# The layer norm of a segment ranked 800 operations later, and the first five weight blocks kept in DRAM like the others

## The chip, the cores and the metric

The kernel runs on one core of a Trainium2 chip. The metric is the device time of one execution in microseconds; several runs are taken and their median is quoted. One more execution was recorded by the hardware profiler, and every row below comes from that one.

## The reference

One layer of a decoder with two token mixers on the same input, for a prompt of 2048 tokens and for 8 short sequences of 4 tokens ("decode"). Cut to what matters here:

```python
u = x * (1 + scale) + shift                 # scale, shift, gate from c @ w_ada
proj = u @ w_in                             # 1024 -> 9344 columns
y_a = rwkv7(proj...)                        # branch A: 16 heads of 64, a recurrent state
y_b = retention(proj...)                    # branch B: 4 heads, chunks of 128 tokens
merged = sigmoid(g_a) * o_a + sigmoid(g_b) * o_b
sub = merged @ w_out
y = norm(ALPHA * x + gate * sub) * ln_gain + ln_bias
```

All data are float32. The last line, with the multiplication of `sub` by `gate`, is the stage whose rank changes.

## The kernel before, in words

**Segments and heads.** The prompt is cut into 4 segments of 512 tokens. A segment begins with `uprep`, which loads x in 8 slices, forms u and splits it into a high part `uh` and a low part `ul` (the products are done in three passes: high by high, high by low, low by high). Segment 1 also carries the 32 decode tokens, so each of its slices is split in three pieces and its matmuls are twice 272 columns. Then come four rounds, one for each retention head. A round does two pairs of heads of branch A (`pair_inputs`, five blocks of projection each; then `half`, `solve`, `half`), one head of branch B (`ret_proj`, two `ret_gate`, `ret_math`), and the output projection of the round before (`outproj`), because the order of a round is `P0 J R G0 D P1 N O G1 S J M00 M01 M10`, with `O` the output projection. `D` is the decode computation, once, in the first round of segment 2.

**Output.** `outproj` adds its products into one buffer, `zt` (128 partitions by 4 by 1024). There is only one `zt`; the first round of the next segment overwrites it in its own output projection (`A.copy(out=z, in_=pz)`, one round after). After the fourth round `outproj` calls `final`: for each half of the columns and each of 4 token blocks GpSimd multiplies `zt` by the gate, VectorE adds the scaled x and takes the statistics; then VectorE normalises, GpSimd multiplies by the gain, VectorE adds the bias, and the rows are stored. That is 16 GpSimd and 32 large VectorE operations and 76 operations in all. Because of the order of a round, the `final` of segments 0, 1 and 2 runs in the first round of segments 1, 2 and 3. The last segment ends with another function, `outproj_last`, which the change does not touch.

**Weights.** A block of `w_in` is loaded as two float32 halves into `fx` buffers (there are 4). ScalarE casts a half to its high part, GpSimd subtracts to get the low part (`split`). The result, 1 MB for a block in a `ww` buffer (3 of them), is stored to DRAM by a transfer on the SP queue (`wpair`, the `cache`) and loaded again in later segments by one transfer that GpSimd issues. Five blocks, `FIRST = 24, 41, 57, 0, 8`, are loaded and split ahead, during the first `uprep` (`ahead`), into buffers of several kinds. These five are not stored in segment 0; segment 1 loads and splits them again and stores them then.

**The order.** All operations are first recorded with a rank, their number in program order plus an offset (`prio_off`; `uprep` of segments 1 to 3 has -700). A planner then lays them out on a model of the engines: whenever an engine is free in the model, it takes the available operation with the lowest rank. It prefers one kind of matmul to another within 500 ranks. The engines execute the resulting lists in order; so do SP's and GpSimd's queues of transfers. Since every instruction is issued from one place, all rows say L529 and must be told apart by tile names.

In program order, the `final` of segment 0 holds operations 9021 to 9096 of 31541; then come `ret_gate`, `ret_math` and the second `half, solve, half` of that round, up to 9750, and `pair_inputs` of the next round. The next overwrite of `zt` is in the `outproj` at 11187. For segment 1 the numbers are 18194 to 18269 and 19866, for segment 2 they are 25296 to 25371 and 26974.

Of the kernel before, what the change touches and what calls it, by code (L numbers as in the profile page):

```python
# [10 lines left out]
F32 = mybir.dt.float32  # L11
# [51 lines left out]
RUN = 2  # L63
UPO = 700
DOFF = 0
JBN = 3, 2, 2, 2, 2
JB=dict(zip(("AR", "W", "UV", "BT", "Z"), JBN))
NPP,NSM = 3,3
# [758 lines left out]
class Mixer:  # L827
# [277 lines left out]
    def proj(self, s, blk, dst, to=None):  # L1105
        dec = s == self.dseg
        n = 2 if dec else 1
        pts = [self.early.pop(blk, None) or self.pp.tile([128, 512], F32, tag="pp", name="pp") for _ in range(n)]
        if (blk, 0) in self.first:
            ws = [self.first.pop((blk, g)) for g in range(2)]  # L1110
        else:
            ws = self.wpair("wf", (blk,), [self.i["wf"][blk, g] for g in range(2)], s < self.ns - 1,
                            to if to is not None and to.t.tag.tag in EARLY else None)
        for g in range(2):
            hi, lo = ws[g]
            for k4 in range(4):
                k = g * 4 + k4
                ks = slice(k4 * 128, (k4 + 1) * 128)
                for q, (w, u) in enumerate(((hi, self.uh), (hi, self.ul), (lo, self.uh))):
                    for j in range(n):  # L1120
                        mv = u[k][:, j * 272:(j + 1) * 272] if dec else u[k][:, 0:512]
                        if to is not None and to.t.tag.tag in LATE and to.t.first is None and k == q == j == 0 and not (s == 0 and blk in FIRST):
                            self.pl.reserve = (to,)
                        self.pl.hold = self.begin if s == 0 and k == 0 and blk in FIRST else None
                        self.T.matmul(pts[j][:, 0:272] if dec else pts[j], lhsT=w[:, ks], rhs=mv,
                                      start=(k == 0 and q == 0), stop=(k == 7 and q == 2))
                        self.pl.hold = None
        if dec:
            t = self.tiny(ND)
            for j in range(2):  # L1130
                self.A.copy(out=t[:, j * 16:(j + 1) * 16], in_=pts[j][:, 256 - 256 * j:272 - 256 * j])
            self.nc.sync.dma_start(out=self.ddram[:, dst], in_=t)
            return [(pts[0][:, 0:256], 0, 256), (pts[1][:, 16:272], 256, 256)]
        return [(pts[0], 0, 512)]
# [673 lines left out]
    def outproj(self, s, h, dec):  # L1808
        T, V, A, G = self.T, self.V, self.A, self.G
        last = s == self.ns - 1  # L1810
        if last and h == NH_B - 1:
            return self.outproj_last(s)
        if h == 0:
            self.zt = self.j1.tile([128, 4, D], F32, tag="zt", name="zt")
        for q in range(4):
            qs = slice(q * 256, (q + 1) * 256)
            if last:
                if q % 2 == 0:
                    wg = self.ww.tile([128, 2, 2, 512], F32R, tag="ww", name="ww")
                hi, lo = self.split(self.i["wo"][h, q], wg[:, q % 2, 0], wg[:, q % 2, 1], gate=q)  # L1820
            else:
                if q % 2 == 0:
                    wp = self.wpair("wo", (h, q), [self.i["wo"][h, q + g] for g in range(2)], s < self.ns - 2)
                hi, lo = wp[q % 2]
            ws = [slice(k * 256, (k + 1) * 256) for k in range(2)]
            for i2 in range(2):
                pz = self.pp.tile([128, 2, 256], F32, tag="pp", name="pp")
                for j in range(2):
                    i = i2 * 2 + j
                    n = 0  # L1830
                    for k in (1, 0):
                        mh, ml = self.mg[k]
                        for w, m in ((hi, mh), (hi, ml), (lo, mh)):
                            T.matmul(pz[:, j], lhsT=m[:, i * 128:(i + 1) * 128], rhs=w[:, ws[k]], start=n == 0, stop=n == 5)
                            n += 1
                z = self.zt[:, 2 * i2:2 * i2 + 2, qs]
                if h == 0 and last:
                    x = self.fx((128, 2, 256))
                    r = s * SEG + i2 * 256
                    self.nc.sync.dma_start(out=x, in_=self.i["xp"][r:r + 256, qs].rearrange("(j p) c -> p j c", j=2))  # L1840
                    V.scalar_tensor_tensor(out=z, in0=x, scalar=ALPHA, in1=pz, op0=MUL, op1=ADD)
                elif h == 0:
                    A.copy(out=z, in_=pz)
                else:
                    V.tensor_tensor(out=z, in0=pz, in1=z, op=ADD)
            if dec:
                self.outproj_dec(h, [(q, (hi, lo))])
        self.mg = {}
        if h == NH_B - 1:
            rows = [slice(s * SEG + i * 128, s * SEG + (i + 1) * 128) for i in range(4)]  # L1850
            self.final([[self.zt[:, i, 0:512], self.zt[:, i, 512:1024]] for i in range(4)], 128,
                       [self.i["xp"][r] for r in rows], [self.o["yp"][r] for r in rows], False)

    def outproj_last(self, s):

# [108 lines left out]
    def run(self):  # L1964
# [3 lines left out]
        for s in range(self.ns):  # L1968
# [8 lines left out]
            for h in range(NH_B):  # L1977
                last = s == self.ns - 1 and h == NH_B - 1
                gate = {}
                for step in (LAST if last else ORDER if s + h else BEGIN).split():  # L1980
# [28 lines left out]
                    elif step[0] == "D" and s == self.dseg + 1 and h == 0:  # L2009
                        self.pl.prio_off = DOFF  # L2010
                        self.decode()
# [28 lines left out]
```

## Time and profile before

| | us |
|---|---|
| median of 3 runs | 3134.05 |
| lowest and highest | 3130.12, 3137.01 |
| the profiled execution | 3128.51 |
| its span, first to last instruction | 3126.7 |

The mean granted TensorE clock over the span is 0.969 of full speed. PE is TensorE's matmuls, DVE is VectorE, ACT ScalarE, POOL GpSimd, SP the queue of transfers. A wait is named by who waited and for what: "PE pp <- DVE t" is TensorE waiting to write an accumulator `pp` until VectorE has written `t`, that is, has read the accumulator out.

### The profile page before, as it was taken

The numbers are of one execution on the slowest core, as the hardware profiler recorded it, in microseconds if no ns is written. First come the engines' busy times: TensorE is split into PE (matmuls) and PEld (weight loads), VectorE is DVE, ScalarE is ACT, GpSimd is POOL, SyncE is SP. The second block draws the span as 40 slices with busy tenths as digits, with TensorE's granted clock in tenths as the row PEclk, the third lists the DMA queues.
The fourth block names the chain that finished last, engine by engine and source line by source line (L and its number), as shares of the span: only waits on it lengthen the run. The fifth ranks groups of instructions, "written<-read, shape, count | busy, mean of one in ns | idle before, by whom it ended". The sixth has DMA issues, their size and how long they took to land. (4 is left out here: it accounts for less than half of the span.)

```text
span 3126.7 us, 63842 instructions
## 1 busy us (share of the span) xinstructions
PE 2896.4 (93%) x24700; PEld 2332.8 (75%) x24700; DVE 1919.9 (61%) x4748; ACT 1566.2 (50%) x3859; POOL 1048.3 (34%) x1451
## 2 busy tenths in 40 slices
PE   8999999989989999989998788999999989998996
PEld 5777778768888989879774466777787766777675
DVE  3566676666576365565665575565676675566666
ACT  4466755656436455453541045554555346454652
POOL 4554456433252131222210242232232442334232
PEclk9999999999999999999998789999999999999997
DMA  8564556534362433425344432333343452533321
GB/s 303 199 229 161 175 191 222 191 127 160 117 226 99 130 108 112 137 94 178 136 128 150 158 110 97 135 124 122 131 152 124 156 176 79 172 119 122 108 83 38
DMA packets 132792, 451.86 MB, mean 145 GB/s; under 512 B 30500, under 2 KB 41636, under 8 KB 92680
## 3 DMA queue, kind: packets, MB, share of 16 engines
q0 software_dynamic: 33120, 241.19, 22.5%
q1 hardware_dynamic: 99368, 206.58, 19.6%
q8 instruction: 195, 3.19, 0.4%
q14 instruction: 109, 0.89, 0.1%
HBM read 345.83 MB, written 101.88 MB: 143 GB/s over the span
## 5 line engine op out<-in xcount | busy, mean ns | idle before, releaser
L529 PE MATMUL pp<-uh,ww 128*128 128x512 f32 (+1 forms) x5152 | 1476.8, 366 | 43.8 <-DMA ww<-wc_wf 15.6
L529 PEld LDWEIGHTS pp<-uh,ww 128*128 128x128 f32 x5152 | 880.5, 190 | 168.3 <-DVE t L529 22.7
L529 PE MATMUL pp<-ul,ww 128*128 128x512 f32 (+1 forms) x2576 | 883.7, 364 | 0.1
L529 PEld LDWEIGHTS pp<-ul,ww 128*128 128x128 f32 x2576 | 468.6, 190 | 54.5 <-issue 1.4
L529 POOL DMA_DIRECT2D ww<-wc_wf x190 | 109.0, 574 | 625.3 <-PE pp L529 514.5
L529 POOL TENSOR_TENSOR ww<-fx,ww 128x512 fp32r<-128x512 f32 x178 | 234.4, 1330 | 211.5 <-ACT ww L529 197.7
L529 ACT CAST ZX<-sm 128x512 f16<-128x512 f32 (+1 forms) x363 | 206.3, 572 | 91.0 <-PE sm L529 86.7
L529 ACT ACTIVATE tn<-UV,PL 64x64 f32<-64x64 f32 x512 | 177.0, 346 | 117.9 <-DVE UV L529 95.8
L529 POOL TENSOR_TENSOR t<-t,t 128x256 fp32r<-128x256 f32 (+2 forms) x160 | 150.6, 943 | 199.5 <-ACT t L529 189.1
L529 DVE TENSOR_TENSOR HH<-sm,lev 128x512 f16<-128x512 f32 (+1 forms) x165 | 111.3, 674 | 160.5 <-PE sm L529 159.7
L529 PE MATMUL pp<-ww,mh 128*128 128x256 f32 x960 | 190.4, 290 | 3.5 <-ACT zt L529 1.9
L529 DVE TENSOR_SCALAR UV<-ch 64x64 f32<-64x64 f32 x256 | 55.2, 227 | 207.3 <-ACT UV L529 184.4
L529 POOL TENSOR_TENSOR tn<-tn,mhalf 128x4 f32<-128x4 f32 (+2 forms) x108 | 100.9, 935 | 216.1 <-DVE tn L529 214.1
L529 PE MATMUL pp<-ww,uh 128*128 128x256 f32 x1024 | 171.6, 291 | 1.4 <-DVE t L529 0.8
L529 ACT CAST bdZ<-sm 64x512 f16<-64x512 f32 (+1 forms) x264 | 149.5, 566 | 24.9 <-PE sm L529 20.1
L529 PEld LDWEIGHTS pp<-ww,mh 128*128 128x128 f32 x960 | 154.9, 193 | 8.0 <-ACT zt L529 2.3
L529 PEld LDWEIGHTS pp<-ww,uh 128*128 128x128 f32 x1024 | 140.7, 190 | 5.3 <-ACT UV L529 0.7
L529 DVE SCALAR_TENSOR_TENSOR UV<-ch,PL,tn 64x64 f32<-64x64 f32 x384 | 108.7, 283 | 57.4 <-PE ch L529 47.5
L529 ACT ACTIVATE t<-pp 128x512 f32<-128x512 f32 (+1 forms) x160 | 80.6, 519 | 118.3 <-PE pp L529 100.7
L529 PE MATMUL pp<-ww,ml 128*128 128x256 f32 x480 | 138.4, 289 | 0.1
L529 ACT ACTIVATE UV<-ch 64x64 f32<-64x64 f32 x256 | 51.6, 215 | 171.3 <-PE yy L529 137.8
L529 DVE COPY bdH<-HH 64x512 f16<-64x512 f16 (+1 forms) x396 | 124.7, 315 | 8.5
(255 smaller groups left out, 5420.1 us busy)
## 6 DMA issues: line engine op xcount, KB each, us to landing
ww<-wc_wf POOLq DMA_DIRECT2D x190, 1024.0 KB, 5.1
wc_wf<-ww SPq DMA_DIRECT2D x65, 1024.0 KB, 5.4
fx<-in_wf SPq DMA_DIRECT2D x140, 256.0 KB, 3.4
ww<-wc_wv POOLq DMA_DIRECT2D x24, 1024.0 KB, 5.2
ww<-wc_wo POOLq DMA_DIRECT2D x16, 1024.0 KB, 5.1
wa<-in_wa SPq DMA_DIRECT2D x16, 512.0 KB, 5.2
wc_wv<-ww SPq DMA_DIRECT2D x8, 1024.0 KB, 5.5
fx<-in_wo SPq DMA_DIRECT2D x32, 256.0 KB, 2.8
```

Of the source, the lines that this page charges most:

```text
L529: op.fn = lambda: real(*[res(x) for x in a], **{k: res(x) for k, x in kw.items()})
```

## The change

The `final` that follows the last output projection of segments 0, 1 and 2 gets 800 added to the rank of each of its operations, its transfers on the SP queue included. And each of the five blocks loaded first is stored to DRAM in segment 0, as four transfers of 256 KB (its halves lie in different buffers), after its matmuls in program order; from segment 1 on it is loaded from there.

```diff
+FOFF = 800
...
-        if (blk, 0) in self.first:
+        early = (blk, 0) in self.first
+        if early:
             ws = [self.first.pop((blk, g)) for g in range(2)]
...
+        if early:
+            key = "wf", blk
+            self.cache[key] = self.drp.tile([128, 2, 2, 512], F32, name="wc_wf_%d" % blk)
+            for g in range(2):
+                for q in range(2):
+                    self.nc.sync.dma_start(out=self.cache[key][:, g, q], in_=ws[g][q].bitcast(F32))
...
         if h == NH_B - 1:
             rows = [slice(s * SEG + i * 128, s * SEG + (i + 1) * 128) for i in range(4)]
+            off, self.pl.prio_off = self.pl.prio_off, FOFF
             self.final([[self.zt[:, i, 0:512], self.zt[:, i, 512:1024]] for i in range(4)], 128,
                        [self.i["xp"][r] for r in rows], [self.o["yp"][r] for r in rows], False)
+            self.pl.prio_off = off
```

## Rows read from the trace of the kernel before

**Rows 1.** The page: busy us, share of the span and instructions of each engine.

```profile
PE 2896.4 (93%) x24700; PEld 2332.8 (75%) x24700; DVE 1919.9 (61%) x4748; ACT 1566.2 (50%) x3859; POOL 1048.3 (34%) x1451
```

**Rows 2.** Stretches: busy us of PE, PEld, DVE, ACT, POOL; PEclk; DMA share, GB/s.

```profile
685.00:715.00 30.00, 15.88 (x88) 13.12 (x87) 28.32 (x69) 15.66 (x32) 15.38 (x20) 0.72 0.50 146
885.00:925.00 40.00, 27.98 (x207) 27.36 (x207) 35.57 (x52) 9.01 (x28) 30.44 (x34) 0.87 0.69 234
1780.00:1840.00 60.00, 39.53 (x246) 31.68 (x245) 52.15 (x96) 21.34 (x42) 38.62 (x40) 0.77 0.47 154
2480.00:2540.00 60.00, 45.60 (x196) 35.84 (x194) 43.80 (x64) 14.14 (x27) 38.20 (x43) 0.89 0.69 228
1455.00:1480.00 25.00, 24.66 (x157) 21.19 (x157) 19.60 (x40) 14.24 (x34) 8.14 (x17) 1.00 0.56 183
```

**Rows 3.** Columns as in rows 2, the stretches whose clock fell furthest.

```profile
700.00:715.00 15.00, 11.84 (x69) 10.50 (x70) 13.79 (x28) 7.92 (x16) 8.19 (x9) 0.59 0.39 101
915.00:920.00 5.00, 2.96 (x13) 2.96 (x14) 4.99 (x10) 1.48 (x2) 3.31 (x3) 0.50 0.36 109
1790.00:1810.00 20.00, 11.80 (x47) 8.60 (x48) 16.09 (x31) 6.07 (x14) 16.66 (x20) 0.55 0.35 117
2520.00:2530.00 10.00, 3.07 (x7) 2.48 (x8) 8.52 (x15) 2.58 (x5) 4.80 (x5) 0.57 1.02 335
```

**Rows 4.** PE's waits, 680-725, 870-935, 1640-1850, 2440-2560 (total, times, longest).

```profile
PE sm L529 <- DVE BK L529: 11.1, 1, 11.1
...
PE pp L529 <- DVE t L529: 10.2, 1, 10.2
...
PE sm L529 <- POOL lw L529: 8.3, 1, 8.3
PE pp L529 <- DVE gate_t L529: 5.0, 1, 5.0
...
PE pp L529 <- DMA ww<-wc_wf: 14.4, 3, 9.3
```

**Rows 5.** Groups by form: the operations of final (busy us, mean ns).

```profile
L529 POOL TENSOR_TENSOR zt<-zt,fx 128x512 f32<-128x512 f32 x48 | 70.6, 1493 | 17.2 <-DMA fx<-gdram 11.0 <-DVE zt L529 5.9
L529 DVE TENSOR_TENSOR zt<-zt,fx 128x512 f32<-128x512 f32 x24 | 28.9, 1245 | 0.1
L529 DVE SCALAR_TENSOR_TENSOR zt<-fx,zt 128x512 f32<-128x512 f32 x24 | 23.3, 985 | 10.8 <-DMA fx<-in_xp 8.8 <-POOL zt L529 2.0
L529 DVE BATCH_NORM_STATS2 tn<-zt 128x6 f32<-128x512 f32 x32 | 21.0, 678 | 0.1
L529 DVE TENSOR_SCALAR zt<-zt,tn 128x512 f32<-128x512 f32 x24 | 19.7, 865 | 1.2 <-POOL tn L529 1.2
```

**Rows 6.** Instructions on zt, second and third final: ns min/median/max, first and last start.

```profile
L529 POOL TENSOR_TENSOR zt<-zt,fx x16: 1257/1396/2487, 1773.1 to 1819.5; 128x512 f32<-128x512 f32 x16
...
L529 POOL TENSOR_TENSOR zt<-zt,fx x16: 1260/1480/1753, 2476.8 to 2521.0; 128x512 f32<-128x512 f32 x16
```

**Rows 7.** Columns as in rows 2, one stretch behind each final.

```profile
950.00:1000.00 50.00, 45.65 (x508) 40.56 (x504) 36.03 (x105) 25.67 (x82) 15.65 (x25) 1.00 0.32 107
1850.00:1900.00 50.00, 46.23 (x376) 33.94 (x376) 32.23 (x91) 26.38 (x76) 15.93 (x28) 1.00 0.31 107
2560.00:2620.00 60.00, 55.57 (x527) 42.97 (x525) 33.44 (x99) 35.44 (x95) 15.34 (x29) 0.97 0.31 104
```

**Rows 8.** Groups by form: the GpSimd half of the splits.

```profile
L529 POOL TENSOR_TENSOR ww<-fx,ww 128x512 fp32r<-128x512 f32 x178 | 234.4, 1330 | 211.5 <-ACT ww L529 197.7 <-DMA t<-in_wg 6.5 <-ACT tn L529 2.9
```

**Rows 9.** Columns as in rows 2, the start of the kernel.

```profile
0.00:45.00 45.00, 35.71 (x221) 18.63 (x221) 11.79 (x29) 16.28 (x28) 16.25 (x17) 1.00 0.95 355
45.00:60.00 15.00, 15.00 (x70) 12.02 (x67) 11.41 (x15) 7.82 (x15) 9.77 (x15) 1.00 0.28 92
```

**Rows 10.** Timeline: the first overwrite of zt in segments 2 and 3.

```profile
1919.51 0.58 ACT L529 COPY zt<-pp 128x512 f32<-128x512 f32 x1
...
2653.75 0.69 DVE L529 SCALAR_TENSOR_TENSOR zt<-fx,pp 128x512 f32<-128x512 f32 x1 [1.95 <-PE pp L529]
```

## Prediction

> **What bounds the kernel now.** I read the page first. TensorE is busy for 2896.4 us, 93% of the span; VectorE has 61% and GpSimd 34% [rows 1]. So TensorE sets the end, and a change can gain in two ways only: where TensorE stands idle, and where it runs at the lower of its two clock levels. What it can give is bounded by the 230 us that are left of the span, less what the change does not reach.
>
> Then I read the stretches in order of time and looked for those in which PE's busy time falls behind the length. Rows 2 show five. Four lose much. Around the `uprep` of segment 1 (685 to 715) PE is idle for 30 − 15.9 = 14.1 us. Around the three `final`s it is idle for 40 − 28.0 = 12.0, 60 − 39.5 = 20.5 and 60 − 45.6 = 14.4 us [rows 2]. The fifth row is for comparison: around the `uprep` of segment 2, which splits no weights, PE loses 0.3 us in 25 [rows 2]. Right behind each idle time the granted clock lies at 0.50 to 0.59, so near 1.2 GHz, and the matmuls in that stretch take up to twice as long [rows 3].
>
> Last, PE's waits, to see who ends the idle time. At the first `final` it is an accumulator that VectorE has not read out (`DVE t`, 10.2 us in one piece). At the second it is a weight that GpSimd has not subtracted (`POOL lw`, 8.3) and another accumulator (`DVE gate_t`, 5.0). At the third it is a block that GpSimd has to fetch (`DMA ww<-wc_wf`, 14.4 in three pieces) [rows 4]. None of these belongs to `final`. They stand behind its operations in the lists of VectorE and GpSimd: in the stretches of rows 2 VectorE is 73 to 89% busy and GpSimd 64 to 76%, against 56 to 72% and 26 to 32% a little later [rows 2, 7]. TensorE works some 700 ranks ahead of `final`: the `t` that it misses at the first one belongs to `pair_inputs` of the next round, at rank 9750 and beyond, against 9021. Such an eviction has the higher rank number, so `final` goes first.
>
> **The change part by part.**
>
> *The first blocks in segment 1.* Five blocks are no longer loaded, cast, subtracted and stored there. That takes away 10 loads of 256 KB and 5 stores of 1 MB from SP, 10 casts from ScalarE and 10 subtractions from GpSimd, 10 × 1.33 = 13.3 us of GpSimd [rows 8]; it adds 5 transfers that GpSimd issues. Only the blocks 24, 0 and 8 fall into the stretch 685 to 715; 41 and 57 fall ahead of the first `final`, where PE is not short, and count as nothing: TensorE's own work covers them. In the stretch PE loses 14.1 us, and the 11.8 us of matmuls at clock 0.59 would take 0.41 × 11.8 = 4.9 less at full clock [rows 2, 3]: 19.0 us in all. The longest wait in it is for VectorE (`DVE BK`, 11.1) [rows 4], which is 94% busy there, also with the decode pieces of `uprep`, which stay. But VectorE is held up by GpSimd's subtractions, and x waits for `fx` buffers that the splits hold. The bounds are 0 (VectorE's own work is the whole loss) and 19.0 (segment 1 becomes like segment 2). I take half, −9.5, since the trace shows both causes and prices neither.
>
> *The first blocks in segment 0.* 20 transfers, 5.24 MB, join the SP queue as soon as their data are there, for the planner takes an available operation whenever SP is free. Until 45 us the DMA engines are 95% busy at 355 GB/s; from 45 to 60 they are 28% busy while PE has 15 of 15 us of work [rows 9]. 5.24 MB at 355 GB/s are 14.8 us. The free DMA time at 45 to 60 is 0.72 × 15 = 10.8 us, and TensorE has matmuls to cover it. If the stores fill just that gap, 4.0 us stay; if all stand ahead of x and the weights with no cover, 14.8. I take +6, near the lower end, since the cover is in the rows. What also waits behind a store on SP are the later weights' loads, and they are part of this delay.
>
> *The `final`s.* Nothing is removed: 48 operations of GpSimd (70.6 us) and 96 large ones of VectorE are to be done as before, 28.9 + 23.3 + 19.7 + 24/32 × 21.0 = 87.7 us, or 29.2 for each `final` [rows 5]. What moves is who waits. Of the next round, `ret_gate`, `ret_math`, `half, solve, half` (up to rank 9750 in segment 1) and the first 70 of `pair_inputs` now go ahead of it; in segments 2 and 3, where rounds are shorter, nearly all of `pair_inputs` does. Its transfers of x and of the gate have the new rank too, but SP is mostly free and takes them as soon as `fx` buffers are. In time: the second `final` starts at 1773.1 [rows 6], and `zt` is next written 1672 ranks on (18194 to 19866) at 1919.5 [rows 10], so 800 ranks are 800/1672 × 146.4 = 70 us; for the third, 800/1678 × 176.9 = 84 us. There VectorE has 28 to 44% of its time free and GpSimd 68% or more [rows 7]; 29.2 us of VectorE fit into 70 to 85 us. What can be saved are the named waits and the slow clock behind them: 10.2 + 0.50 × 3.0 = 11.7 us at the first, 8.3 + 5.0 + 0.45 × 11.8 = 18.6 at the second, 14.4 + 0.43 × 3.1 = 15.7 at the third, 46.0 in all [rows 3, 4]. The bounds are 0 and 46.0. I take half, −23: the free time is there, but the lists are executed in order, and one operation of `final` in a wrong place still stops an eviction behind it. The `fx` buffers, too, are held 70 to 85 us longer; nothing else needs them then, except the weights of `outproj` in segment 3, a rival below.
>
> *Sum.* −9.5 + 6 − 23 = −26.5 us. Against the profiled execution's 3128.51 that is 3102.0. That execution lies 5.5 below the median of the runs shown, so I put the same difference to the median: 3134.05 − 26.5 = 3107.5.
>
> **The rivals.**
>
> *The stalls move along.* `final` takes as much of VectorE and GpSimd wherever it lies. For it: VectorE's operations with two operands in SBUF take 1245 and 985 ns while GpSimd multiplies, where the statistics with one operand of the same size take 678 [rows 5], so (1245 − 678) × 24 + (985 − 678) × 24 = 21 us of VectorE are lost to GpSimd, and they go along. The Trainium skill, in "SBUF — State Buffer", section "Who interferes with whom", makes this a rule that speaks against the change: a VectorE instruction with two SBUF inputs and a GpSimd instruction that reads SBUF exclude each other for a whole instruction, wherever they meet. By that rule the 21 us are a property of `final` and not of its place; the trace agrees with its 1245 against 678 ns [rows 5]. Against it: the work that would stand behind it has passed by then. It gives no gain from the `final`s: −9.5 + 6 = −3.5, so 3130.5.
>
> *`zt` comes free too late.* The first write of the next round (1919.5 in segment 2, 2653.7 in segment 3 [rows 10]) then waits for `final`'s last stores, with ScalarE's or VectorE's list behind it, and the accumulators of the projections fill up. The last GpSimd operations on `zt` start at 1819.5 and 2521.0 [rows 6] and some 5 us more finish a `final` (an estimate: four operations of rows 5 and a store); 70 and 84 us later is 1895 and 2610, which leaves 25 and 44 us. It decides from the point where `final` runs that much longer than now, in segment 3 sooner if `fx` buffers held by it also delay the weights. Priced like the costliest stretch, 19.0 us each: −26.5 + 38 = +11.5, so 3145.5, slower. Against it: these writes have higher ranks than `final`.
>
> *Everything comes back.* −19.0 − 46.0 + 4.0 = −61.0, so 3073.
>
> **How the numbers follow.** This kernel's measurement tells about 0.2%, 6.3 us, from no change. My forecast (a gain between 6.3 and some 50) gets 0.60, everything back 0.08, the stalls that move along 0.14, the late `zt` 0.11. For a loss of another kind I keep 0.07, since the new ranks lay out all lists anew behind the first stores. So faster 0.68, same 0.14, slower 0.18. The likeliest case alone runs from −9.5 − 46 + 4 = −51.5 (all of the `final`s) to 0 − 15 + 6 = −9 (a third of them, and nothing in `uprep`), 3082.5 to 3125. The range over all cases goes from a little below that, 3078, to the late `zt`, 3145.5.
>
> **What would show it right or wrong.** Right: in the stretches where `final` lay, PE is busy nearly throughout at clock 1.00, and `DVE t`, `POOL lw`, `gate_t` and `ww<-wc_wf` leave the list of PE's waits; `zt<-zt,fx` on GpSimd starts some 70 to 85 us later and spread wider; PE loses under 10 us around `uprep` of segment 1, where no `ww<-fx` stands; the end of the first five blocks, near 60 us, comes some 6 us later. Wrong: PE has an idle piece of 5 us or more behind a run of `zt` operations in the new place; a wait for `zt` at the next round's first write; waits for `wa` or x at the start above 7 us more than now; or `uprep` of segment 1 losing as much as before, with VectorE full.

## The result, and the profile after

The changed kernel takes 3100.16 us (median of 4 runs, 3094.76 to 3101.70) against 3134.44 for the kernel before (4 runs, 3130.12 to 3137.01). The ratio is 0.9889, 95% interval 0.9872 to 0.9906: faster by 34.3 us, where 26.5 were forecast. The profiled execution took 3094.76 us with a span of 3093.0, 33.7 less than before.

The page after; it answers to rows 1:

```profile
PE 2897.4 (94%) x24700; PEld 2335.1 (75%) x24700; DVE 1908.6 (62%) x4748; ACT 1560.7 (50%) x3849; POOL 1025.7 (33%) x1446
```

TensorE is as busy as before (2897.4 against 2896.4 us [rows 1]). The span less PE's busy time fell from 230.3 to 195.6, by 34.7 us, so between these two profiles the whole gain is idle time of TensorE.

The same stretches as in rows 2, of the changed kernel:

```profile
685.00:715.00 30.00, 23.26 (x145) 19.05 (x143) 23.06 (x71) 14.78 (x33) 12.66 (x22) 1.00 0.70 237
885.00:925.00 40.00, 38.39 (x339) 37.04 (x338) 32.19 (x60) 15.81 (x47) 24.81 (x38) 1.00 0.68 225
1780.00:1840.00 60.00, 55.50 (x506) 44.20 (x508) 53.97 (x108) 29.20 (x65) 27.91 (x30) 0.94 0.53 182
2480.00:2540.00 60.00, 57.02 (x542) 44.64 (x538) 55.56 (x118) 29.61 (x69) 27.81 (x34) 0.99 0.62 207
```

The first column behind the length is PE. Around the three `final`s it now loses 1.6, 4.5 and 3.0 us, where it lost 12.0, 20.5 and 14.4 [rows 2], and the clock there is 1.00, 0.94 and 0.99. VectorE (the third figure) is a little less full at the first (32.19 us against 35.57) and fuller at the other two (53.97 against 52.15, 55.56 against 43.80). Around `uprep` of segment 1 PE loses 6.7 us where it lost 14.1.

PE's waits after, in 680 to 725, 870 to 960, 1760 to 1900 and 2440 to 2560 us, the longest of each (total, times, longest); they answer to rows 4:

```profile
PE sm L530 <- DVE BK L530: 2.9, 1, 2.9
...
PE pp L530 <- DVE gate_t L530: 2.1, 1, 2.1
...
PE pp L530 <- DVE t L530: 1.5, 1, 1.5
...
PE sm L530 <- DVE BK L530: 4.2, 1, 4.2
...
PE sm L530 <- DVE BK L530: 7.0, 3, 6.3
```

The waits of 10.2, 8.3, 5.0 and 14.4 us at the `final`s are gone. What is left at the second and third is `DVE BK` (4.2 and 7.0 us), an input of the own round's `half`; at the second it was 0.8 us before, at the third none.

Where the 33.7 us came from is read from landmarks of the two traces. The first write of `zt` in segment 0 comes at 324.8 us instead of 318.8: +6.0 for the start. From there to the first GpSimd operation of the first `final` (876.3 instead of 876.1) it is 551.5 instead of 557.3: −5.8 for segment 0's remainder and `uprep` of segment 1. From that operation to the end of the span it is 2216.7 instead of 2250.6: −33.9 for the rest, with the three `final`s in it. The middle one is steady: that stretch takes 550.7 to 553.7 us in the profiles of all eleven kernels of this text that have the stores, and 556.5 to 557.3 in the three that have not. The +6.0 is not steady; more on it with the stores at the start.

**Where `final` now lies.** Its operations by form (busy us, mean ns), which answer to rows 5, and those of the second `final` on GpSimd (ns min/median/max, first and last start), which answer to rows 6:

```profile
L530 POOL TENSOR_TENSOR zt<-zt,fx 128x512 f32<-128x512 f32 x48 | 63.6, 1342 | 27.6 <-DVE zt L530 24.5 <-DMA fx<-gdram 2.8
L530 DVE SCALAR_TENSOR_TENSOR zt<-fx,zt 128x512 f32<-128x512 f32 x24 | 24.8, 1050 | 8.8 <-DMA fx<-in_xp 6.1 <-POOL zt L530 2.7
L530 DVE BATCH_NORM_STATS2 tn<-zt 128x6 f32<-128x512 f32 x32 | 21.5, 683 | 0.2
L530 DVE TENSOR_TENSOR zt<-zt,fx 128x512 f32<-128x512 f32 x24 | 19.5, 834 | 0.2
```

```profile
L530 POOL TENSOR_TENSOR zt<-zt,fx x16: 1260/1282/1528, 1766.8 to 1843.2; 128x512 f32<-128x512 f32 x16
```

It does not start later: 1766.8 against 1773.1 [rows 6], in a kernel that is some 8 us ahead by then. It is spread wider, over 76 us instead of 46. The other two take 67 instead of 40 and 72 instead of 44.

**What the spread changes** is seen in VectorE's timeline at the first `final`. Before (start, us, operation, count):

```profile
900.25 2.66 DVE L529 TENSOR_SCALAR zt<-zt,tn 128x512 f32<-128x512 f32 x3 [0.23 <-POOL tn L529]
903.05 3.87 DVE L529 TENSOR_TENSOR zt<-zt,fx 128x512 f32<-128x512 f32 x3
906.84 2.96 DVE L529 TENSOR_SCALAR zt<-zt,tn 128x512 f32<-128x512 f32 x3
909.72 4.55 DVE L529 TENSOR_TENSOR zt<-zt,fx 128x512 f32<-128x512 f32 x3
914.19 0.99 DVE L529 TENSOR_SCALAR zt<-zt,tn 128x512 f32<-128x512 f32 x2
915.10 1.48 DVE L529 TENSOR_TENSOR AR<-t,t 128x256 f32<-128x256 f32 x1
916.51 1.26 DVE L529 SCALAR_TENSOR_TENSOR t<-pp,omu,t 128x256 f32<-128x256 f32 x3
```

After:

```profile
905.61 0.85 DVE L530 SCALAR_TENSOR_TENSOR BK<-t,t 64x256 f32<-64x256 f32 x2
906.49 0.88 DVE L530 SCALAR_TENSOR_TENSOR t<-pp,omu,t 128x256 f32<-128x256 f32 x2
...
909.89 0.95 DVE L530 TENSOR_SCALAR zt<-zt,tn 128x512 f32<-128x512 f32 x1 [0.78 <-POOL tn L530]
910.76 0.68 DVE L530 TENSOR_TENSOR W<-sm,cst 128x512 f32<-128x512 f32 x1
...
913.70 1.06 DVE L530 TENSOR_TENSOR zt<-zt,fx 128x512 f32<-128x512 f32 x1
914.68 0.41 DVE L530 TENSOR_TENSOR AR<-t,t 128x256 f32<-128x256 f32 x1
```

Before, 14 large operations of `final` stood in one run from 900.25 to 915.1, and behind them `AR`, an input of the own round's `half`, and the eviction `t<-pp,omu,t` at 916.5, ten microseconds later than after the change. Now they stand one at a time between `BK`, `W` and `AR`.

**What is left.** The 6.3 us of `DVE BK` at the third `final` are in PE's, VectorE's and GpSimd's timelines of the changed kernel:

```profile
2478.01 1.12 PE L530 MATMUL sm<-cst,BK 128*128 128x128 f32 x4 [6.28 <-DVE BK L530]
```

```profile
2469.37 0.69 DVE L530 SCALAR_TENSOR_TENSOR zt<-fx,zt 128x512 f32<-128x512 f32 x1 [4.13 <-DMA fx<-in_xp]
2469.98 0.42 DVE L530 TENSOR_TENSOR AR<-t,t 128x256 f32<-128x256 f32 x1
...
2473.39 4.56 DVE L530 TENSOR_TENSOR BK<-t,t 64x256 f32<-64x256 f32 x2
```

```profile
2473.53 3.70 POOL L530 TENSOR_TENSOR zt<-zt,fx 128x512 f32<-128x512 f32 x3
```

An operation of `final` waited 4.13 us for its x with `AR` right behind it in VectorE's list. Then two `BK` operations took 4.56 us together, while three multiplications of `final` ran on GpSimd one behind the other; the median of such a `BK` is 421 ns, the longest 4128.

### The profile page after: what moved, and what is told of

Its sections match the earlier page's. It is cut to its first block, busy times and chain, and to the rows that moved or that the text cites. A ratio compares the mean times of both kernels' runs of the same rounds, so it can differ in the third digit from the quotient of the medians.

```text
span 3093.0 us, 63845 instructions
## 1 busy us (share of the span) xinstructions
PE 2897.4 (94%) x24700; PEld 2335.1 (75%) x24700; DVE 1908.6 (62%) x4748; ACT 1560.7 (50%) x3849; POOL 1025.7 (33%) x1446
## 5 line engine op out<-in xcount | busy, mean ns | idle before, releaser
L530 PE MATMUL pp<-uh,ww 128*128 128x512 f32 (+1 forms) x5152 | 1485.2, 367 | 18.8 <-DVE t L530 6.0
L530 PEld LDWEIGHTS pp<-uh,ww 128*128 128x128 f32 x5152 | 884.2, 190 | 143.5 <-DVE uh L530 5.8
L530 PE MATMUL pp<-ul,ww 128*128 128x512 f32 (+1 forms) x2576 | 885.9, 364 | 0.6 <-DVE ul L530 0.5
L530 PEld LDWEIGHTS pp<-ul,ww 128*128 128x128 f32 x2576 | 469.9, 190 | 55.6 <-issue 2.0
L530 POOL DMA_DIRECT2D ww<-wc_wf x195 | 112.2, 575 | 655.7 <-PE pp L530 529.7
L530 POOL TENSOR_TENSOR ww<-fx,ww 128x512 fp32r<-128x512 f32 x168 | 221.5, 1331 | 199.3 <-ACT ww L530 194.8
L530 ACT CAST ZX<-sm 128x512 f16<-128x512 f32 (+1 forms) x363 | 206.4, 572 | 108.2 <-PE sm L530 103.8
L530 ACT ACTIVATE tn<-UV,PL 64x64 f32<-64x64 f32 x512 | 176.9, 346 | 117.8 <-DVE UV L530 103.4
L530 POOL TENSOR_TENSOR t<-t,t 128x256 fp32r<-128x256 f32 (+2 forms) x160 | 150.2, 939 | 198.7 <-ACT t L530 187.0
L530 DVE TENSOR_TENSOR HH<-sm,lev 128x512 f16<-128x512 f32 (+1 forms) x165 | 111.2, 674 | 163.5 <-PE sm L530 162.7
L530 PE MATMUL pp<-ww,mh 128*128 128x256 f32 x960 | 192.6, 292 | 2.4 <-DVE t L530 0.7
L530 POOL TENSOR_TENSOR tn<-tn,mhalf 128x4 f32<-128x4 f32 (+2 forms) x108 | 101.0, 936 | 237.9 <-DVE tn L530 236.3
L530 DVE TENSOR_SCALAR UV<-ch 64x64 f32<-64x64 f32 x256 | 55.1, 227 | 194.7 <-ACT UV L530 175.5
L530 PE MATMUL pp<-ww,uh 128*128 128x256 f32 x1024 | 171.3, 290 | 0.7 <-DVE t L530 0.7
L530 ACT CAST bdZ<-sm 64x512 f16<-64x512 f32 (+1 forms) x264 | 149.5, 566 | 31.2 <-PE sm L530 27.1
L530 PEld LDWEIGHTS pp<-ww,mh 128*128 128x128 f32 x960 | 155.6, 193 | 6.8 <-DVE t L530 1.0
L530 DVE SCALAR_TENSOR_TENSOR UV<-ch,PL,tn 64x64 f32<-64x64 f32 x384 | 108.7, 283 | 57.4 <-PE ch L530 47.7
L530 PEld LDWEIGHTS pp<-ww,uh 128*128 128x128 f32 x1024 | 139.9, 190 | 4.6 <-DVE t L530 1.6
L530 ACT ACTIVATE UV<-ch 64x64 f32<-64x64 f32 x256 | 51.6, 215 | 179.8 <-PE yy L530 145.8
L530 PE MATMUL pp<-ww,ml 128*128 128x256 f32 x480 | 138.9, 290 | 0.1
L530 ACT ACTIVATE t<-pp 128x512 f32<-128x512 f32 (+1 forms) x160 | 80.5, 520 | 107.0 <-PE pp L530 91.3
L530 DVE COPY bdH<-HH 64x512 f16<-64x512 f16 (+1 forms) x396 | 129.1, 326 | 8.6 <-PE sm L530 0.3
```

What stands on the lines that cost most here:

```text
L530: op.fn = lambda: real(*[res(x) for x in a], **{k: res(x) for k, x in kw.items()})
```

## The experiments

All have the changed kernel as their base, so the edits are against it. Ratios are to the kernel before. Their profiles name the one line L530 or L531.

**The two parts alone.** The first leaves out the stores, the second the offset.

```diff
-        if early:
-            key = "wf", blk
...
```

> The offset of 800 alone, without the stores in segment 0. Main theory (the operations of the final stood ahead of evictions and weights in the in-order lists): nearly the whole gain, 26 to 40 us below the kernel before, so 3094 to 3108; the uprep of segment 1 loses as much as before, the start is as fast as before (first write of zt near 318.8). Rival (the parts need each other, or the gain is a chance of the new lists): less than 15 us.

```diff
-FOFF = 800
+FOFF = 0
```

> The stores of the five first blocks alone, offset 0. Main theory: about 6 us lost at the start and about as much won back around the uprep of segment 1 (predicted 9.5, seen in the trace of the changed kernel 5.6), so 3128 to 3137, within 0.2% of before, with PE's idle time at the three finals still there. Rival (the stores carry the gain, for instance by freeing fx buffers and GpSimd in segment 1): 3120 or less.

The offset alone: 3092.64 us, 0.9864 (0.9838 to 0.9889). The stores alone: 3135.36, 1.0004 (0.9990 to 1.0018). So the offset carries the gain, and the stores are worth −3 to +6 us, which no measurement here tells from nothing. With the stores alone the start costs 6.1 us (324.9 against 318.8) and the stretch from there to the first `final` gives 4.9 back (552.4 against 557.3); PE's longest wait at `uprep` of segment 1 is as in the changed kernel. With the offset alone it is as before (680 to 725 us of each):

```profile
PE sm L530 <- DVE BK L530: 11.1, 1, 11.1
```

```profile
PE sm L530 <- DVE BK L530: 2.9, 1, 2.9
```

The first line is the offset alone, the second the stores alone: the missing splits took 8.2 us from that wait, and the stretch gained 4.9.

**How much offset is needed.** The prediction put the stall on an eviction some 700 ranks away. With 400 the `final` of segment 0 still begins at rank 9421, ahead of the next round's 9750; with 1500 it lies far behind.

```diff
-FOFF = 800
+FOFF = 400          # and 1500, 100, 250 in three others
```

> Both parts, with an offset of 400 in place of 800. Main theory: 400 ranks end inside the solve of the same round, so the final still stands ahead of the next round's projections, which are 730 ranks away; it gives half of the gain of the offset or less: 3108 to 3125. Rival (it is enough that the final is behind the gates of its own round, or the gain is chance): within 6 us of 3100, or no order at all.

> Both parts, with an offset of 1500: in segments 2 and 3 the final then ranks some 170 ahead of the next write of zt. Main theory: evictions and weights are still ahead, so the finals cost no more than at 800, unless the zt buffer comes free too late: 3095 to 3110 if it doesn't, and a wait for zt at the first write of the next round (near 1903 and 2614 us) with 3115 or more if it does. Rival (chance of the new lists): anywhere between 3090 and 3140, with no wait for zt.

> Both parts with an offset of 100. The offset of 400 gave the whole gain, so the next round's projections (730 ranks away) can't be what had to go ahead. New theory: it is the own round's gate, retention and first half, which end 236 to 294 ranks behind the start of the final. Then 100, which is behind the gate in segments 2 and 3 only and within it in segment 1, gives half of the gain or less: 3112 to 3130. Rival (any offset is enough, as it only breaks up the run of zt operations): 3090 to 3103.

> Both parts with an offset of 250, which is behind the own round's first half in segments 2 and 3 and within it in segment 1. New theory: nearly the whole gain, 3092 to 3106. Rival (the solve's operations, up to 600 ranks, are what matters): 3110 or more.

| offset, with the stores | us | ratio | 95% |
|---|---|---|---|
| 0 | 3135.36 | 1.0004 | 0.9990 to 1.0018 |
| 100 | 3137.58 | 1.0013 | 1.0000 to 1.0025 |
| 250 | 3117.39 | 0.9946 | 0.9930 to 0.9962 |
| 400 | 3093.18 | 0.9873 | 0.9857 to 0.9890 |
| 800 | 3100.16 | 0.9889 | 0.9872 to 0.9906 |
| 1500 | 3092.25 | 0.9873 | 0.9858 to 0.9888 |

The last three are three different lists and all lie at 0.987 to 0.989, so the gain is not the chance of one new list. From 400 I had expected half of the offset's gain or less, and from 100 some of it; 400 gives the whole gain and 100 none.

With 100 all four waits are there. PE's waits in 870 to 960, 1760 to 1900 and 2440 to 2560 us:

```profile
PE pp L530 <- DVE t L530: 10.3, 1, 10.3
...
PE sm L530 <- POOL lw L530: 8.6, 1, 8.6
PE pp L530 <- DVE gate_t L530: 5.3, 1, 5.3
...
PE pp L530 <- DMA ww<-wc_wf: 14.2, 3, 8.0
```

With 250 the first `final` is clear (no wait over 1.8 us), and the others have these, in 1760 to 1900 and 2440 to 2560:

```profile
PE sm L530 <- DVE bdH L530: 6.8, 3, 5.2
PE sm L530 <- DVE BK L530: 3.7, 2, 3.1
...
PE pp L530 <- DMA ww<-wc_wf: 4.2, 1, 4.2
```

I had expected nearly the whole gain from 250; it is half. `bdH` belongs to `solve`. So operations of `final`'s own round, the inputs of `half` and a part of `solve`, have to go ahead of it: at 250 TensorE still waits for them.

Whether the next round's evictions have to pass `final` as well is not settled by the 400, for there they do pass in part. VectorE's timeline with 400, at the first `final` (start, us, operation, count):

```profile
904.72 0.88 DVE L530 SCALAR_TENSOR_TENSOR t<-pp,omu,t 128x256 f32<-128x256 f32 x2 [0.28 <-POOL t L530]
905.51 0.86 DVE L530 TENSOR_SCALAR zt<-zt,tn 128x512 f32<-128x512 f32 x1
...
914.56 0.86 DVE L530 SCALAR_TENSOR_TENSOR t<-pp,omu,t 128x256 f32<-128x256 f32 x2
...
916.98 0.68 DVE L530 TENSOR_TENSOR zt<-zt,fx 128x512 f32<-128x512 f32 x1
```

Two pairs of evictions stand ahead of pieces of `final` that have the lower rank. The planner has a rule that the description of the order leaves out: where its model has GpSimd busy and VectorE's next operation reads two inputs from SBUF, or is a copy or a `tensor_scalar` there, VectorE takes instead the lowest-ranked available operation that does neither, if it lies fewer than 600 ranks further on (`DWIN = 600`). From the operations of `final` (9021 to 9096, plus the offset) to 9750, where the next round begins, it is 254 to 329 ranks with 400, 404 to 479 with 250, 554 to 629 with 100 and 654 to 729 with no offset. So with 250 and 400 an eviction may pass, with no offset it may not, and 100 lies at the edge. Both readings, the own round's operations and the evictions that this rule lets by, fit the first `final`, and no run here sets them apart.

The prediction's late `zt` does not come. With 1500 the last GpSimd operation of the second `final` starts at 1857.2 and `zt` is first overwritten at 1890.3, with no wait for it.

**The same gain from 400 without the stores:**

```diff
-FOFF = 800
+FOFF = 400
...
-        if early:
-            key = "wf", blk
...
```

> The offset alone, at 400, without the stores. The two that gave the whole gain in one: if the stores bring nothing beside the offset (as they did by themselves), 3088 to 3097. If they bring their 5 us around the uprep of segment 1 without a cost at the start: 3096 to 3102.

3095.83 us, 0.9876 (0.9860 to 0.9892): again the whole gain.

**Which engine's list.** The offset is given to VectorE's operations of `final` alone, or to GpSimd's and its transfers on SP alone; the stores stay.

```diff
-        op.prio = op.num + self.prio_off
+        op.prio = op.num + (self.prio_off if self.off_for is None or eng in self.off_for else 0)
...
+            self.pl.off_for = ("DVE",)      # the other: ("POOL", "SP")
```

> Both parts, the offset of 800 only for VectorE's operations of the final; GpSimd's and the transfers keep their old rank. If the late evictions on VectorE are the stall: the first final loses nothing any more, and the third, where TensorE waited for a transfer that GpSimd issues, keeps some 10 us: 3105 to 3118. If GpSimd's list is the stall: 3120 or more.

> Both parts, the offset of 800 only for GpSimd's operations and the transfers of the final; VectorE's keep their old rank but depend on GpSimd's. If VectorE's list is the stall: the run of zt operations on VectorE stays at the first final with a PE wait of 5 us or more: 3108 to 3125. If GpSimd's list is the stall, or paces the final: 3092 to 3104.

VectorE alone: 3100.38 us, 0.9896 (0.9874 to 0.9918), the whole gain within the intervals, though PE keeps 7.6 us for `DVE t` at the second `final`, the longest 5.3. GpSimd and SP alone: 3148.69, 1.0050 (1.0031 to 1.0068), slower by 15.7 us (0.0050 of 3134), beyond both cases that I had set down for it. The two halves are not quite apart: the multiplications by the gain, half of GpSimd's operations in a `final`, take VectorE's result and so come later with VectorE's offset too. I had expected the third `final`'s wait for a block fetched by GpSimd to outlast VectorE's offset; it is 0.6 us there. In the slower one the second `final` has the worst wait, PE's in 1760 to 1900, and VectorE's timeline shows a part of it:

```profile
PE sm L531 <- DVE BK L531: 15.0, 2, 14.1
```

```profile
1801.01 0.88 DVE L531 TENSOR_TENSOR AR<-t,t 128x256 f32<-128x256 f32 x1
1801.81 0.20 DVE L531 BATCH_NORM_AGGREGATE tn<-tn 128x2 f32<-128x12 f32 x1
1801.93 2.23 DVE L531 SCALAR_TENSOR_TENSOR zt<-fx,zt 128x512 f32<-128x512 f32 x2
1804.08 1.27 DVE L531 BATCH_NORM_STATS2 tn<-zt 128x6 f32<-128x512 f32 x2
...
1806.61 0.52 DVE L531 SCALAR_TENSOR_TENSOR BK<-t,t 64x256 f32<-64x256 f32 x1
```

VectorE's operations kept their rank, so as soon as GpSimd has multiplied a piece, the addition of x and the statistics go ahead of `BK`: 4.8 us between `AR` and `BK`, with TensorE waiting. The rest of the 14.1 us is not taken apart here; two of the four `BK` operations also take a product that GpSimd began only at 1806.95.

**The stores at the start.** One kernel stores each first block twice, to another buffer; the other lets a block's stores begin only when its last matmul is done.

```diff
+            twice = self.drp.tile([128, 2, 2, 512], F32, name="wd_wf_%d" % blk)
...
+                    self.nc.sync.dma_start(out=twice[:, g, q], in_=ws[g][q].bitcast(F32))
```

> The changed kernel with each of the five first blocks stored twice in segment 0, 5.24 MB more that nobody reads. If the start is bound by the transfers and its cover of 10.8 us is used up by the first copy (the prediction's step): 10 to 15 us slower than the changed kernel's 3100, so 3110 to 3116, the first write of zt near 336. If the stores fit into free time of the DMA engines and of TensorE: within 5 us of 3100, first write of zt below 328.

```diff
+            self.pl.hold = self.pl.ops[-1]
             self.cache[key] = ...
...
+            self.pl.hold = None
```

> The changed kernel with the stores of a first block held until its last matmul, so that they leave the saturated first 45 us. If their place ahead of x and the weights is what costs at the start: first write of zt back near 319 to 321, 3094 to 3099. Rival (they only move into the stretch from 60 to 95 us, in which the DMA engines were 94% busy before, and hold two of the three ww buffers longer): first write of zt at 325 or later, 3098 to 3108.

Stored twice: 3105.18 us, 0.9909 (0.9893 to 0.9926). The first write of `zt` comes at 331.8, another 7.0 later than after the change, between the two cases that I had set down (below 328 and near 336). Held: 3092.97, 0.9865 (0.9849 to 0.9881), with that write at 321.1. The start of the changed kernel, the lines that answer to rows 9, and two of PE's waits in 0 to 100 us:

```profile
0.00:45.00 45.00, 36.83 (x214) 20.58 (x214) 10.97 (x21) 14.21 (x24) 13.99 (x15) 1.00 0.98 361
45.00:60.00 15.00, 10.96 (x55) 7.13 (x51) 5.26 (x10) 3.61 (x6) 6.63 (x9) 0.89 1.05 350
```

```profile
PE sm L530 <- DMA wa<-in_wa: 6.7, 3, 5.8
PE pp L530 <- DVE uh L530: 4.1, 2, 2.5
```

And of the version with held stores:

```profile
0.00:45.00 45.00, 36.82 (x226) 19.44 (x227) 11.96 (x29) 16.99 (x29) 17.15 (x18) 1.00 0.94 359
45.00:60.00 15.00, 15.00 (x68) 12.09 (x67) 11.23 (x16) 7.27 (x13) 7.48 (x15) 1.00 0.97 326
60.00:95.00 35.00, 30.21 (x236) 18.82 (x235) 16.27 (x26) 19.89 (x45) 19.56 (x25) 0.90 0.91 320
```

In the changed kernel the stores go ahead of x, and PE loses 4.0 us in 45 to 60 (0 before [rows 9]), 4.1 waiting for `uh`. Held, they fill the DMA time that was free in 45 to 60 (0.97 now, 0.28 before [rows 9]) and PE has 15.00 of 15 there, but loses 4.8 in 60 to 95, where the kernel before lost 2.2.

**The two together,** held stores and an offset of 400:

```diff
-FOFF = 800
+FOFF = 400
...
+            self.pl.hold = self.pl.ops[-1]
```

> The first blocks' stores held till the last matmul of their block, and the offset at 400 instead of 800. If the two gains are independent, the start is as in the version with held stores and 800 (first write of zt of segment 0 near 321 instead of 324.8), the three final stretches are clean as with 400, and the time is 3089 to 3093 us, the lowest of all versions. If neither the place of the stores nor 400 against 800 is worth anything that can be measured, it is 3093 to 3100, within the intervals of the versions with the whole gain. A ratio above 0.990 would say that the two disturb each other.

3091.56 us, 0.9864 (0.9847 to 0.9880). The median is the lowest of all, but the intervals of the held version with 800 and of 400 with unheld stores hold it, and the first write of `zt` came at 323.9, not 321. So neither of these is a better version that this measurement can tell: what is common to all the fast ones is an offset of at least 400 for VectorE's part. The start's cost stays unsettled. Over the profiles with single stores that write lies between 320.0 (offset 100) and 325.2 (offset 400), without stores at 318.8, 320.8 and 321.2: the two groups overlap, so single profiles give anything from nothing to some 6 us. Among the kernels that were run together with the offset alone (320.8), the stores alone, 400 and 1500 have 324.9, 325.2 and 324.1, 3 to 4 us later.

## Why the prediction was right, and which of its steps were not

*What bounds the kernel.* Right: the gain is idle time of TensorE in the four stretches named, and the four named waits at the `final`s went.

*The `final`s, −23 as half of 46.0.* The term was too small; half was a choice for want of a price. Measured are −33.9 in the landmarks, −35 between the stores alone and both parts (3135.36 − 3100.16), and −42.6 for the offset alone (1 − 0.9864, of 3134). Most of the 46.0 came back. It came out near the forecast of the whole partly by luck: the `final`s gave at least 10.9 more than was put down, `uprep` some 4 less. The reason given against taking more, one operation of `final` in a wrong place, was real but small: it is the 6.3 us at the third `final`, which is also the one idle piece of over 5 us that was named as a sign of being wrong. Of the part put on the clock, the stretches themselves show it back at 0.94 to 1.00. PE's busy time in the sum does not show it: 2896.4 before, 2897.4 after. But it is 2908.2 with the stores alone and 2890.2 with 400 and no stores, so one pair of profiles can't tell 10 us of it; from the stores alone to both parts it fell by 10.8 and the idle time by 30.3.

*Why it is gained.* That the work which TensorE waits for stands behind `final` in VectorE's list is right: the timeline before has `AR` and an eviction behind 14 operations of it. The step that failed is the one from there to the ranks: TensorE some 700 ahead, its eviction behind `final` for its higher rank, and so 800 as the number that gets past it. An offset of 400 leaves `final` at the lower rank and gives the whole gain. What the text left out is that the own round's `half` and `solve` have to go first on VectorE too: at 250 TensorE waits for `bdH` and `BK`, and in the kernel with GpSimd's offset alone 14.1 us for `BK`. It also left out the planner's rule of 600 ranks, by which evictions pass `final` at 400 all the same; how much of the gain is theirs stays open. What fits all runs: a run of `final`'s operations on VectorE held back `AR`, `BK` and `W`; TensorE had no solve work, went ahead to the next projections, and filled its accumulators; the late eviction was the last link. At the third `final` the link lay on GpSimd, as the prediction has it: before, four of `final`'s multiplications ran there from 2512.6 to 2518.6, and the fetches of `ww<-wc_wf` were issued behind them; with VectorE's offset alone 0.6 us of that wait are left. That the rank of `final`'s VectorE operations carries the gain is shown by the two half versions; the middle of the chain, TensorE running ahead for lack of solve work, is read from timelines and not isolated.

*When it runs, "70 to 85 us later".* Wrong by the starts (876.3 and 1766.8), right on "spread wider". An offset says what goes first among ready operations; where nothing else is ready, a late rank still runs at once.

*The stores at the start, +6.* Measured +6.0 and +6.1 in two profiles, by the mechanism named (stores ahead of x, 4.1 us for `uh`). That the size fits is partly luck: against the same 318.8 the other profiles with single stores have 1.2 to 6.4, and two kernels without stores 2.0 and 2.4. The bound of 4.0 assumed that PE's work covers the gap at 45 to 60; with the stores issued early it was PE that lost just those 4.0.

*`uprep` of segment 1, −9.5 as half of 19.0.* Measured −5.8 and −4.9, inside the bounds, and the half was too much. The splits had 8.2 of the 11.1 us of `DVE BK`, and TensorE got a part of them; which of their loads, casts and subtractions it was is not isolated. PE loses 6.7 us there now, under the 10 named.

*The rivals.* The stalls did not move along, but for the waits on `BK` (4.2 and 7.0 us). Of the 21 us that VectorE loses to GpSimd in the two-operand operations of `final`, some 9 went: the same sum is now (834 − 683) × 24 + (1050 − 683) × 24 = 12.4 us, 12.5 with the offset alone, and 19.6 with the stores alone. VectorE's total can't be used for it: its 4748 instructions took 1919.9 us before [rows 1] and 1908.6 after, but also 1909.5 with the stores alone. `BK` and `AR`, which now lie between the pieces of `final`, took 205.9 us before and 206.7 after. So the loss is a property of what lies beside what, not of `final` alone. The rule of the Trainium skill, "SBUF — State Buffer", section "Who interferes with whom", that such a VectorE instruction and a GpSimd instruction exclude each other, agrees with the `BK` of 4128 ns; that the whole 21 us would go along does not come out of the runs. The late `zt` did not come even with 1500. Everything back would have been 3073; no median here lies below 3091.

## What to carry to other kernels

Where an engine with free time still stalls the bounding one, look at what stands in a run in its list ahead of small operations that others need: giving the run a later rank, so that it goes in singly, returned here some 34 to 43 of the 46 us that its stalls and the slow clock behind them were reckoned at, with no work removed. Sweep the offset before explaining it: the value at which the gain sets in (here between 100 and 400, not 700) narrows down the operations that must pass. Then look for other rules of the planner that let operations pass at that value; here one reaches 600 ranks. Move a stage's rank on the engine that holds the others up; moved on its producer alone, it cost 15.7 us.

## What was not expected of the hardware

A small VectorE operation can lose far more than one GpSimd instruction lasts: a `BK` of 64x256 with both inputs in SBUF, 421 ns at the median, took 4128 ns while three GpSimd multiplications ran without a gap between them (3.70 us together). With the offset alone the same place has 4133 ns; the longest such `BK` before took 1523. And the same operations became cheaper by being spread: `zt<-zt,fx` on VectorE from 1245 [rows 5] to 834 ns, on GpSimd from 1493 [rows 5] to 1342, with the same counts and shapes, while `zt<-fx,zt` went from 985 [rows 5] to 1050.
